# Two SwiGLU layers by seven block products: another order at the start of the second half's rows, and one set of slots for both phases

## The chip, the cores and the metric

One Trainium2 chip, one core of it. The metric is device time of one execution in microseconds (us); several runs give a median. The profile is one further execution, recorded by the hardware profiler; its times count from the start of its span.

## The reference

Two layers over a sequence of 1024 rows of 1024 features, batch 1, float32. Layer 0 mixes tokens by a gated delta rule, layer 1 by dilated windowed attention; each mixer and each FFN is preceded by an RMS norm with adaLN shift, scale and gate computed from `c`. The change touches the FFN of both layers:

```
def swiglu(h, w_in, w_out):
    gate, up = jnp.split(h @ w_in, 2, axis=-1)
    return (jax.nn.silu(gate) * up) @ w_out
```

with `FFN_HIDDEN` 2816 (22 tiles of 128), so `w_in` is 1024 x 5632 and `w_out` 2816 x 1024. The result is added to `x` under the gate of the adaLN.

## The kernel before, in words

A product of float32 numbers is made of three TensorE passes: each operand is split into a part `hi` (rounded to the matmul's type, a copy on ScalarE) and a part `lo` (the rest, a subtraction by `lo_of`, L164, given in turn to VectorE and GpSimd), and hi·hi, hi·lo and lo·hi are summed in PSUM. `hl` and `hx` are split rows, `w`, `wo` split weights.

**FFN-in.** The sequence is cut in two halves of 512 rows, the features (k) in 8 tiles of 128. For each hidden tile `i` of 22 the gate and the up columns times both halves would be eight block products of 4 k-tiles; the class `FfnIn` forms them from seven, in Winograd's way, `product(i, x)` with x = 1 to 7. Each is 4 k-tiles by 3 passes, 12 matmuls of 128x512. x = 1 and 2 need the first half's rows alone and the plain gate columns; x = 3 needs the plain second half (its k-tiles 4 to 7) and x = 4 to 7 need sums and differences of rows of both halves (`B[4]` to `B[7]`), which `half1` makes. The weights of x = 3, 5, 6, 7 are sums and differences of the raw columns (`weights`, L1209 to L1221), then split (`op`: ScalarE L1192, `lo_of` L164).

`begin` issues (0,1), (0,2), (1,1), (1,2). Then the second half's norm factor is made (a small matmul `pt`, VectorE L347, GpSimd L142, the broadcast matmul `pt`, the ScalarE copy `rb` L306) and `half1` multiplies the 8 k-tiles of the second half by it (L1156), applies the affine step on ScalarE (L1157), and forms `B[7]` (L1170, L1171), `B[6]` (L1176, L1178), `B[5]`, `B[3]`, `B[4]` in that order. `rest` then issues the products: 7, 6, 5 of tiles 0 and 1, then (0,3), (0,4), (2,1), (1,3), (1,4), then for each further tile 7, 6, 2, 5, next tile's 1, 3, 4. The order on TensorE within `begin` and `rest` is that of the program (`PE.pinned`); elsewhere a scheduler sets it, and every engine's queue, SP's DMA issues among them, runs in order.

`taken` gathers each product out of PSUM (L1244 to L1261), and the finished activations go to DRAM, `a_d`. In layer 0 `rest` calls `mods1` after nearly every product: it loads one 256 KB piece of layer 1's adaLN weights (`araw<-in_w_ada`, L226) and accumulates it on VectorE (L230).

**FFN-out.** `ffn_out` takes the hidden tiles in groups `FG` of 3, 4, 4, 4, 4, 3. For each group it loads the activations from `a_d` (L1289), splits them (`hl`, L1291), loads and splits `w_out` rows (`wunit`: L186 to L190, `w`), and makes 16 accumulations `pd` of 3 matmuls per tile of the group, each added to `x` by L1301. In both layers the pools of FFN-in (`hx` 12 buffers, `fw` 6 of `wo`, `ft`) are closed before those of FFN-out are opened, and all 16 tiles of `x` are loaded first (L1368 in layer 0).

Of the kernel before, what the change touches and what calls it, by code (L numbers as in the profile page):

```python
# [17 lines left out]
P = 128  # L18
# [53 lines left out]
def trunk(tc, A, out, stop=None):  # L72
# [236 lines left out]
    def make_h(p, l, w, xs, rb, aid=False, bufs=2):  # L309

        hs = []
        for k in range(KT):
            t = p.tile([P, HALF], F32, name="ht", tag="ht", bufs=bufs)
# [149 lines left out]
    class OutProj:  # L463
# [51 lines left out]
        def late(self, tp, w_from):  # L515
# [8 lines left out]
            stat = Stat(None, *(tp.tile([P, HALF], F32, name="sq", tag="ft") for _ in range(2)))  # L524
# [596 lines left out]
    class Slotted:  # L1121


        def __init__(self, p):
            self.p = p

        def take(self):
            return self.p.tile([P, HALF], F32, name="ft", tag="ft")
# [4 lines left out]
    class FfnIn:  # L1133
# [31 lines left out]
        def half1(self, xs, rb):  # L1165
            x0, x1, ft = self.x0, xs, self.ft
            for k in range(4):
                self.h(k, x1[k], rb)
                self.h(k + 4, x1[k + 4], rb)
                V.tensor_tensor(x0[k], x1[k], x0[k], ALU.subtract)  # L1170
                V.tensor_tensor(x1[k], x1[k + 4], x1[k], ALU.subtract)  # L1171
                self.B[7].append(self.pair(x1[k], True))
                ft.give(x1[k])
            for k in range(4):
                t = ft.take()
# [3 lines left out]
                ft.give(t)  # L1179
            for x, far, ts in ((5, True, x0[:4]), (3, False, x1[4:]), (4, False, x0[4:])):  # L1180
# [15 lines left out]
        def weights(self, i, x):  # L1196
            s, ft = self.st[i], self.ft
            if x in (1, 2):
                if x == 1:
                    s["rg"], s["ru"] = self.raw(i * P), self.raw(HID + i * P)  # L1200
                    w = s["w"] = wps.tile([P, 2, 1024], F32R, name="w", tag="w")
                    ACT.activation(w[:, 0], s["rg"], AF.Copy)
                    lo_of(w[:, 1], s["rg"], w[:, 0])
                c = slice((x - 1) * HALF, x * HALF)
                return s["w"][:, 0, c], s["w"][:, 1, c]
            a11, a12, a21, a22 = (t[:, j * HALF:(j + 1) * HALF] for t in (s["rg"], s["ru"]) for j in range(2))
            if x == 7:
                t = ft.take()
                V.tensor_tensor(t, a11, a21, ALU.subtract)  # L1209
                r = self.op(t)  # L1210
                ft.give(t)
            elif x == 6:
                s["s1"], s["s2"] = ft.take(), ft.take()
                G.tensor_tensor(s["s1"], a21, a22, ALU.add)
                V.tensor_tensor(s["s2"], s["s1"], a11, ALU.subtract)
                r = self.op(s["s2"])
            elif x == 5:
                r = self.op(s["s1"])
                ft.give(s["s1"])
            elif x == 3:  # L1220
                V.tensor_tensor(s["s2"], a12, s["s2"], ALU.subtract)  # L1221
                r = self.op(s["s2"])
                ft.give(s["s2"])
            else:
                r = self.op(a22)
            return r

        def product(self, i, x):
            s = self.st[i]
            wh, wl = self.weights(i, x)  # L1230
            key = {2: "y", 4: "v", 7: "v"}.get(x, "u")
            first, last = x in (1, 2, 7), x in (2, 3, 4)
# [7 lines left out]
        def taken(self, i, x, b):  # L1240
            s, ft = self.st[i], self.ft
            if x in (1, 6, 5):
                t = s["t%d" % x] = ft.take()
                ACT.activation(t, b, AF.Copy)  # L1244
                if x == 5:
                    V.tensor_tensor(t, s["v"], t, ALU.add)  # L1246
            elif x == 2:
# [3 lines left out]
            elif x == 3:  # L1251
                g = ft.take()
                ACT.activation(g, b, AF.Silu)
                G.tensor_tensor(s["t5"], s["t5"], g, ALU.mult)
                SP.dma_start(a_d[i, 1], s["t5"])
                ft.give(g, s["t5"])
# [7 lines left out]
        def begin(self):  # L1264
            for i in range(2):
                for x in (1, 2):
                    self.product(i, x)

        def rest(self, between=None):
            seq = [(i, x) for x in (7, 6, 5) for i in range(2)] + [(0, 3), (0, 4), (2, 1), (1, 3), (1, 4)]  # L1270
            for i in range(2, NHT):
                seq += [(i, 7), (i, 6), (i, 2), (i, 5)] + [(i + 1, 1)] * (i + 1 < NHT) + [(i, 3), (i, 4)]
# [7 lines left out]
    def ffn_out(l, xT, act_raw, tail):  # L1280

        w_o = A["w_ffn_out"][l]
        t0 = 0
        for gi, gn in enumerate(FG):
            wo, acts = [], [[], []]
            for t in range(t0, t0 + gn):
                for hf in range(2):
                    r = act_raw()
# [3 lines left out]
                    lo_of(lo, r, hi)  # L1292
                    acts[hf].append((hi, lo))
                wo.append(wunit(w_o[t * P:(t + 1) * P, None, :], 1))
            for hf in range(2):
                for n in range(KT):
                    o = pd()
                    split3(o, [((wo[i][0][:, 0, n * P:(n + 1) * P], wo[i][1][:, 0, n * P:(n + 1) * P]), acts[hf][i])
                               for i in range(gn)])
                    xt = xT[hf][n]  # L1300
                    V.scalar_tensor_tensor(xt, o, modT[:, l, 5, n:n + 1], xt, op0=ALU.mult, op1=ALU.add)  # L1301
                    if gi == len(FG) - 1:
                        tail(hf, n)
            t0 += gn

# [5 lines left out]
    def attn_weights(g, hq, kind):  # L1311
# [416 lines left out]
```

## Time and profile before

| | |
|---|---|
| median of 3 runs | 3078.36 us (3076.47 to 3082.93) |
| the profiled execution's own time | 3078.52 us |
| its span | 3076.7 us |
| mean granted TensorE clock | 0.945 |
| TensorE busy | 2793.5 us, 91% |
| VectorE, ScalarE, GpSimd busy | 53%, 34%, 32% |
| FFN-in, layer 0 and layer 1 | starts 850.77 and 2339.75, last product starts 1351.64 and 2809.05 |

The page of the profile gives busy time by engine and in 40 slices of the span, the granted TensorE clock of each slice (`PEclk`; 1.00 is 2.4 GHz, 0.50 is 1.2 GHz), the costliest groups of instructions and the DMA issues. The timeline lists consecutive instructions of one group on one engine: start, length, what they do, how many, and in brackets how long the engine stood idle before and what ended that. The end of a matmul is modelled, so the length of a PE row can reach past the next row's start; start to start is the safer reading. The windows view gives busy times, clock and DMA rate of a stretch, the waits view the idle time of an engine by what ended it. In the windows a bracket holds a count of instructions.

### The profile page before, as it was taken

What the parts mean: (1) busy time and instruction counts of PE and PEld (TensorE: products, weight loads), DVE (VectorE), ACT (ScalarE), POOL (GpSimd) and SP (SyncE); (2) the same over time, 40 slices, a digit from 0 to 9 for tenths busy, and PEclk for the clock granted to TensorE, in tenths of its full rate; (3) what the DMA queues carried; (4) which work ended last, traced back from release to release, by engine and by line L of the source; (5) the groups of instructions that cost most, each with busy time, mean ns of one, the idle gap of its engine ahead of it and who ended that gap; (6) DMA issues with size and microseconds to landing.
All of it is one profiled execution on the core that took longest, in us unless ns stands there. A gap on an engine that the chain in (4) does not pass through costs nothing.

```text
span 3076.7 us, 40439 instructions
## 1 busy us (share of the span) xinstructions
PE 2793.5 (91%) x15303; PEld 2372.6 (77%) x15303; DVE 1624.3 (53%) x3040; ACT 1058.5 (34%) x2097; POOL 995.9 (32%) x839
## 2 busy tenths in 40 slices
PE   6889888898949999969999999999975899998999
PEld 5777777776737787858889899999964688887887
DVE  7775576556666666435456342333377644344443
ACT  5432333333442333332124453443335333333210
POOL 2142323421253333433223132222224544444220
PEclk7989899999979999989999999999977999999999
DMA  7334332135705454244222411111231222226211
GB/s 250 97 94 120 95 86 66 55 101 187 236 25 159 148 164 154 83 162 136 79 79 65 107 42 35 50 49 47 80 107 58 82 83 82 82 90 213 95 52 55
DMA packets 301311, 311.78 MB, mean 101 GB/s; under 512 B 35011, under 2 KB 217539, under 8 KB 301116
## 3 DMA queue, kind: packets, MB, share of 16 engines
q1 hardware_dynamic: 293548, 289.30, 30.6%
q0 software_dynamic: 7568, 19.89, 2.0%
q8 instruction: 120, 1.97, 0.3%
q14 instruction: 75, 0.61, 0.1%
HBM read 250.16 MB, written 63.66 MB: 102 GB/s over the span
## 4 chain that ended last, share of the span: by engine, by line
PE 62%; DMA 11%; DVE 10%; POOL 6%; issue 4%; ACT 3%; SPq 0%; DVEq 0%; POOLq 0%; ACTq 0%
PE pd L82 33%; PE u L82 11%; PE v L82 5%; PE pt L82 4%; DMA araw<-in_w_ada 4%; PE y L82 3%; PE ob L82 2%; POOL U L805 2%; POOL Ut L803 2%; DVE acc L230 2%; DMA wraw<-in_gdn_w_in 1%; PE pp L82 1%; PE p L82 1%; DMA E<-gs_d 1%; PE sc L82 1%
## 5 line engine op out<-in xcount | busy, mean ns | idle before, releaser
L82 PE MATMUL pd<-hl,w 128*128 128x512 f32 x4248 | 1082.9, 409 | 53.9 <-ACT hl L1291 24.8
L82 PEld LDWEIGHTS pd<-hl,w 128*128 128x128 f32 x4248 | 807.2, 196 | 223.0 <-ACT hl L1291 25.6
L82 PE MATMUL pd<-w,hl 128*128 128x256 f32 x2880 | 377.4, 287 | 0.0
L82 PEld LDWEIGHTS pd<-w,hl 128*128 128x128 f32 x2880 | 355.8, 192 | 7.2 <-issue 5.9
L164 POOL TENSOR_TENSOR w<-wraw,w 128x1024 fp32r<-128x1024 f32 (+1 forms) x102 | 201.3, 1975 | 358.2 <-ACT w L190 247.4
L190 ACT ACTIVATE w<-wraw 128x512 fp32r<-128x512 f32 (+1 forms) x229 | 159.1, 710 | 299.2 <-DMA wraw<-in_gdn_w_in 98.2
L82 PE MATMUL u<-hx,wo 128*128 128x512 f32 x1056 | 255.7, 392 | 6.4 <-ACT wo L1192 4.5
L82 PEld LDWEIGHTS u<-hx,wo 128*128 128x128 f32 x1056 | 199.0, 189 | 49.1 <-ACT wo L1192 5.0
L164 DVE TENSOR_TENSOR w<-wraw,w 128x512 fp32r<-128x512 f32 (+1 forms) x160 | 154.5, 969 | 132.7 <-ACT w L190 117.2
L82 PE MATMUL v<-hx,wo 128*128 128x512 f32 x528 | 137.5, 411 | 81.0 <-ACT wo L1192 63.5
L82 PEld LDWEIGHTS v<-hx,wo 128*128 128x128 f32 x528 | 103.6, 199 | 108.1 <-ACT wo L1192 65.3
L230 DVE SCALAR_TENSOR_TENSOR acc<-araw,vecT,acc 128x512 f32<-128x512 f32 x140 | 133.9, 956 | 81.3 <-DMA araw<-in_w_ada 80.5
L82 PE MATMUL u<-hl,wo 128*128 128x512 f32 x528 | 129.7, 395 | 12.0 <-ACT ft L1244 8.2
L142 POOL TENSOR_TENSOR ssa<-ssa,pw 128x8 f32<-128x8 f32 x48 | 81.0, 1690 | 171.5 <-DVE ssa L1478 160.9
L1301 DVE SCALAR_TENSOR_TENSOR qkv<-pd,modT,qkv 128x512 f32<-128x512 f32 x96 | 71.5, 748 | 116.4 <-PE pd L82 116.2
L82 PE MATMUL u<-hl,w 128*128 128x512 f32 x528 | 127.2, 390 | 1.8 <-DVE qkv L490 1.8
L82 PE MATMUL v<-hl,wo 128*128 128x512 f32 x528 | 127.5, 391 | 0.7 <-DVE qkv L1246 0.7
L82 PE MATMUL y<-hl,w 128*128 128x512 f32 x528 | 127.1, 390 | 0.0
L82 PEld LDWEIGHTS u<-hl,wo 128*128 128x128 f32 x528 | 99.0, 189 | 36.3 <-ACT ft L1244 10.5
L1301 DVE SCALAR_TENSOR_TENSOR xt<-pd,modT,xt 128x512 f32<-128x512 f32 x96 | 71.2, 747 | 95.5 <-PE pd L82 95.1
L691 DVE SCALAR_TENSOR_TENSOR yv<-raw,vecT,yv 128x512 f32<-128x512 f32 x144 | 111.7, 776 | 12.9 <-ACT yv L689 11.7
L82 PEld LDWEIGHTS u<-hl,w 128*128 128x128 f32 x528 | 98.9, 188 | 22.6 <-issue 2.1
(364 smaller groups left out, 4321.4 us busy)
## 6 DMA issues: line engine op xcount, KB each, us to landing
araw<-in_w_ada SPq DMA_DIRECT2D x160, 256.0 KB, 2.8
wraw<-in_w_ffn_in SPq DMA_DIRECT2D x66, 512.0 KB, 4.3
wraw<-in_w_ffn_out SPq DMA_DIRECT2D x36, 512.0 KB, 4.5
wraw<-in_dsw_w_in SPq DMA_DIRECT2D x72, 256.0 KB, 2.8
wraw<-in_gdn_w_in SPq DMA_DIRECT2D x66, 256.0 KB, 2.9
a_d<-ft SPq DMA_DIRECT2D x44, 256.0 KB, 2.3
ar<-a_d SPq DMA_DIRECT2D x44, 256.0 KB, 4.9
qkv<-in_w_ffn_in SPq DMA_DIRECT2D x22, 512.0 KB, 4.0
```

Of the source, the lines that this page charges most:

```text
L82: i = f(*a, **k)
L142: G.tensor_tensor(o, i, pw[:, half, :n], ALU.pow)
L164: e.tensor_tensor(o, x, hi.bitcast(F32), ALU.subtract)
L190: ACT.activation(hi, raw, AF.Copy)
L230: V.scalar_tensor_tensor(acc, raw, condT[:, k:k + 1], acc, op0=ALU.mult, op1=ALU.add)
L691: V.scalar_tensor_tensor(yv, raw[:, i:i + HALF], convT[:, i, ct:ct + 1], yv, op0=ALU.mult, op1=ALU.add)
L803: G.tensor_tensor(t, U[:, 0:m, m:m + 1].to_broadcast([64, m, n]), U[:, m:m + 1, m + 1:32].to_broadcast([64, m, n]), ALU.mult)
L805: G.tensor_tensor(U[:, 0:m, m + 1:32], U[:, 0:m, m + 1:32], t, ALU.add)
L1301: V.scalar_tensor_tensor(xt, o, modT[:, l, 5, n:n + 1], xt, op0=ALU.mult, op1=ALU.add)
```

## The change

1. `begin` takes over the second half's norm and a third pair of products, (2,1) and (2,2), issued before any that needs the second half. The norm's first matmul comes after (1,2), the broadcast of its factor after (2,1). The gate columns for (2,1) come by a load of their own (`wr`, L1209 of the new file, into a `wo` slot).
2. The weights of (0,3), (1,3), (0,7), (1,7) are formed and split ahead of the second half's rows. The two weight sums `s1`, `s2` of a tile share a slot (`ss`, tag `wo`); differences of weights and rows use `sums` slots (layer 0: the 2 slots `araw`, which the adaLN pieces use too; layer 1: 5 slots `st`).
3. `half1` handles k-tiles 4 to 7 first and forms `B[3]` from them at once; the differences into `x0` move from VectorE (L1170 before) to GpSimd (L1177).
4. `rest` begins with (0,3), (1,3), each alone in its PSUM bank and held in SBUF until x = 5 is there, then 7, 6, 5, 4 of tiles 0 and 1. `mods1` is called after every second product only and goes on in `ffn_out`.
5. One pair of pools serves both phases: `fw` 16 buffers of `wo` (12 of them are the split rows `hx`, the rest are `op`, `ss`, `wr` and later the split `w_out`, as two 128x512 pieces by `wtwo`), `ft` 22. `x` is loaded tile by tile in the first group of `ffn_out`. `FG` becomes 2, 4, 4, 4, 4, 4. The number of matmuls and the bytes loaded stay as they were.

The diff, cut to its core:

```
         def half1(self, xs, rb):
...
+            for k in range(4, KT):
+                self.h(k, x1[k], rb)
+                self.B[3].append(self.pair(x1[k], False))
             for k in range(4):
                 self.h(k, x1[k], rb)
-                self.h(k + 4, x1[k + 4], rb)
-                V.tensor_tensor(x0[k], x1[k], x0[k], ALU.subtract)
-                V.tensor_tensor(x1[k], x1[k + 4], x1[k], ALU.subtract)
-                self.B[7].append(self.pair(x1[k], True))
+                t = sums.take()
+                V.tensor_tensor(t, x1[k + 4], x1[k], ALU.subtract)
+                self.B[7].append(self.pair(t, True))
+                sums.give(t)
+                G.tensor_tensor(x0[k], x1[k], x0[k], ALU.subtract)
...
-            for x, far, ts in ((5, True, x0[:4]), (3, False, x1[4:]), (4, False, x0[4:])):
+            for x, far, ts in ((5, True, x0[:4]), (4, False, x0[4:])):
...
+                    if i == 2:
+
+                        r = self.fw.tile([P, 1024], F32, name="wr", tag="wo")
+                        SP.dma_start(r.rearrange("p (k n) -> p k n", k=KT),
+                                     rows_cols(A["w_ffn_in"][self.l], i * P, P))
...
+            if x in (6, 5, 3) and "s1" not in s:
+                t = self.fw.tile([P, 2, HALF], F32, name="ss", tag="wo")
+                s["s1"], s["s2"] = t[:, 0], t[:, 1]
...
-        def begin(self):
-            for i in range(2):
-                for x in (1, 2):
-                    self.product(i, x)
+        def begin(self, factors, bcast):
+
+            for i in range(3):
+                self.product(i, 1)
+                if i == 2:
+                    rb = bcast(r)
+                self.product(i, 2)
+                if i == 1:
+                    r = factors()
+                    for j in ((0, 3), (1, 3), (0, 7), (1, 7)):
+                        self.ops[j] = self.weights(*j)
+            return rb
 
         def rest(self, between=None):
-            seq = [(i, x) for x in (7, 6, 5) for i in range(2)] + [(0, 3), (0, 4), (2, 1), (1, 3), (1, 4)]
+            seq = [(i, x) for x in (3, 7, 6, 5, 4) for i in range(2)]
...
-                if between is not None and n >= 8:
+                if between is not None and n >= 8 and n % 2:
                     between()
 
-    FG = [3, 4, 4, 4, 4, 3]
+    FG = [2, 4, 4, 4, 4, 4]
...
-            fw = f1.enter_context(pool("fw", 6))
-            tp = f1.enter_context(pool("ft", 18))
...
+        fw = fa.enter_context(pool("fw", 16))
+        tp = fa.enter_context(pool("ft", 22))
```

TensorE's queue at the start of layer 0's second half. Before:

```order
L82 MATMUL y<-hl,w 128x512 x12
L82 MATMUL pt<-sq 128x1 x4
L82 MATMUL pt<-sq,rst 128x128 x4
L82 MATMUL v<-hx,wo 128x512 x24
L82 MATMUL u<-hx,wo 128x512 x48
L82 MATMUL u<-hl,wo 128x512 x12
L82 MATMUL v<-hl,wo 128x512 x12
L82 MATMUL u<-hl,w 128x512 x12
```

And in the changed kernel:

```order
L82 MATMUL y<-hl,w 128x512 x12
L82 MATMUL pt<-sq 128x1 x4
L82 MATMUL u<-hl,w 128x512 x12
L82 MATMUL pt<-sq,ssx 128x128 x4
L82 MATMUL y<-hl,w 128x512 x12
L82 MATMUL y<-hl,wo 128x512 x24
L82 MATMUL v<-hx,wo 128x512 x24
L82 MATMUL u<-hx,wo 128x512 x48
```

The broadcast of the factor (`pt<-sq,ssx`) now stands behind (2,1) (`u<-hl,w`), and (2,2), (0,3), (1,3) (`y`) stand ahead of the first product that needs a difference of rows (`v<-hx,wo`).

SP's queue of DMA issues in the changed kernel, at the same place (`wraw` are the raw gate and up columns of hidden tiles 0, 0, 1, 1, 2, 2 in turn):

```order
L1193 DMA wraw_7276<-in_w_ffn_in 128x8x128
L1193 DMA wraw_7278<-in_w_ffn_in 128x8x128
L1193 DMA wraw_7313<-in_w_ffn_in 128x8x128
L1193 DMA wraw_7315<-in_w_ffn_in 128x8x128
L1193 DMA wraw_7707<-in_w_ffn_in 128x8x128
L1193 DMA wraw_7709<-in_w_ffn_in 128x8x128
L1209 DMA wr_7383<-in_w_ffn_in 128x8x128
L226 DMA araw_7704<-in_w_ada 128x512
```

There are four buffers of `wraw`, so the fifth and the sixth load wait until the sums of tile 0 have been formed on VectorE; the load `wr` that (2,1) needs stands behind both. VectorE's queue there (`araw` here holds a difference of weights):

```order
L1263 TENSOR_TENSOR ft<-y,ft 128x512
L1229 TENSOR_TENSOR araw<-wraw,ss 128x512
L164 TENSOR_TENSOR wo<-araw,wo 128x512
L1229 TENSOR_TENSOR araw<-wraw 128x512
L1263 TENSOR_TENSOR ft<-y,ft 128x512
L347 TENSOR_SCALAR ssx<-pt 128x4
L1229 TENSOR_TENSOR araw<-wraw 128x512
L164 TENSOR_TENSOR wo<-araw,wo 128x512
L1157 TENSOR_TENSOR xt<-xt,rb 128x512 x8
```

The last of these differences, that of (1,7), stands behind the norm's L347.

## Rows read from the trace of the kernel before

**Rows 1.** The page: busy time by engine, 40 slices, the granted clock.
```profile
PE 2793.5 (91%) x15303; PEld 2372.6 (77%) x15303; DVE 1624.3 (53%) x3040; ACT 1058.5 (34%) x2097; POOL 995.9 (32%) x839
PEclk7989899999979999989999999999977999999999
```

**Rows 2.** Timeline of PE, layer 0: start us, length, instruction, count [idle before <-releaser].
```profile
863.98 1.16 PE L82 MATMUL pt<-sq,rst 128*128 128x128 f32 x8 [1.38 <-POOL rst L142]
890.23 1.22 PE L82 MATMUL v<-hx,wo 128*128 128x512 f32 x2 [25.10 <-ACT wo L1192]
900.71 7.81 PE L82 MATMUL v<-hx,wo 128*128 128x512 f32 x22 [9.26 <-POOL wo L164]
908.36 2.88 PE L82 MATMUL u<-hx,wo 128*128 128x512 f32 x12
915.78 10.27 PE L82 MATMUL u<-hx,wo 128*128 128x512 f32 x36 [4.55 <-ACT wo L1192]
...
939.58 0.61 PE L82 MATMUL v<-hx,wo 128*128 128x512 f32 x2
```

**Rows 3.** Windows, layer 0's start: us, then busy us by engine, PEclk, DMA share, GB/s.
```profile
860.00:870.00 10.00, 3.76 (x24) 3.17 (x23) 5.05 (x9) 5.29 (x9) 1.68 (x2) 0.76 0.00 0
880.00:890.00 10.00, 0.00 (x0) 0.00 (x0) 10.00 (x9) 6.66 (x12) 8.17 (x6) 0.50 0.00 0
```

**Rows 4.** Timeline of VectorE, layer 0.
```profile
862.64 0.16 DVE L347 TENSOR_SCALAR rst<-pt 128x4 f32<-128x4 f32 x1 [5.11 <-PE pt L82]
865.80 5.98 DVE L1156 TENSOR_TENSOR xt<-xt,rb 128x512 f32<-128x512 f32 x8 [1.84 <-ACT rb L306]
...
878.06 0.68 DVE L1170 TENSOR_TENSOR xt<-xt 128x512 f32<-128x512 f32 x1
...
887.76 3.43 DVE L1209 TENSOR_TENSOR ft<-wraw 128x512 f32<-128x512 f32 x2
...
899.46 1.74 DVE L164 TENSOR_TENSOR wo<-ft,wo 128x512 fp32r<-128x512 f32 x1
```

**Rows 5.** Timeline of PE, layer 1.
```profile
2353.07 1.85 PE L82 MATMUL pt<-sq,ssx 128*128 128x128 f32 x8 [1.37 <-POOL ssx L142]
2385.49 1.22 PE L82 MATMUL v<-hx,wo 128*128 128x512 f32 x2 [30.57 <-ACT wo L1192]
...
2428.70 2.88 PE L82 MATMUL v<-hx,wo 128*128 128x512 f32 x12
```

**Rows 6.** Timeline of PE, from FFN-in to FFN-out: layer 0, then layer 1.
```profile
1378.58 10.98 PE L82 MATMUL pd<-hl,w 128*128 128x512 f32 x36 [24.06 <-ACT hl L1291]
...
2817.28 7.48 PE L82 MATMUL pd<-hl,w 128*128 128x512 f32 x24 [5.35 <-ACT w L190]
2825.47 1.19 PE L82 MATMUL pd<-hl,w 128*128 128x512 f32 x4 [0.72 <-ACT hl L1291]
2827.98 3.59 PE L82 MATMUL pd<-hl,w 128*128 128x512 f32 x8 [1.32 <-POOL hl L164]
2832.53 17.77 PE L82 MATMUL pd<-hl,w 128*128 128x512 f32 x77 [0.96 <-DVE qkv L1301]
```

**Rows 7.** Windows, FFN-in of both layers past its start, and layer 0's change of phase.
```profile
905.00:1352.00 447.00, 425.75 (x1875) 348.02 (x1875) 260.96 (x325) 143.75 (x237) 173.01 (x107) 0.98 0.42 129
2430.00:2809.00 379.00, 375.18 (x1651) 309.51 (x1651) 152.10 (x193) 133.09 (x214) 152.21 (x96) 1.00 0.29 92
1380.00:1390.00 10.00, 9.84 (x35) 7.63 (x34) 7.19 (x7) 7.79 (x12) 9.37 (x5) 0.80 1.04 396
```

**Rows 8.** DMA issues of the page: count, KB each, median us to landing.
```profile
wraw<-in_w_ffn_in SPq DMA_DIRECT2D x66, 512.0 KB, 4.3
```

**Rows 9.** Groups of instructions in 905 to 1352 us: count | busy us, mean ns.
```profile
L164 POOL TENSOR_TENSOR w<-wraw,w 128x1024 fp32r<-128x1024 f32 x20 | 48.9, 2446 | 84.1 <-ACT w L1202 74.2 <-DMA araw<-in_w_ada 5.3 <-DMA wraw<-in_w_ffn_in 4.6
L1202 ACT ACTIVATE w<-wraw 128x1024 fp32r<-128x1024 f32 x20 | 21.2, 1061 | 60.7 <-DMA wraw<-in_w_ffn_in 43.7 <-PE y L82 17.0
L230 DVE SCALAR_TENSOR_TENSOR acc<-araw,vecT,acc 128x512 f32<-128x512 f32 x84 | 91.0, 1083 | 44.4 <-DMA araw<-in_w_ada 43.8
```

More of the change, by code (lines that the diff above doesn't have):

```diff
@@ L523, in late @@
             rb0 = row_bcast(tp, self.r0, bufs=1)
-            stat = Stat(None, *(tp.tile([P, HALF], F32, name="sq", tag="ft") for _ in range(2)))
+            stat = Stat(None, *(tp.tile([P, HALF], F32, name="sq", tag="araw", bufs=2) for _ in range(2)))
             for n in range(KT):
@@ L1229, in product @@
             s = self.st[i]
-            wh, wl = self.weights(i, x)
+            wh, wl = self.ops.pop((i, x), None) or self.weights(i, x)
             key = {2: "y", 4: "v", 7: "v"}.get(x, "u")
-            first, last = x in (1, 2, 7), x in (2, 3, 4)
+            alone = i < 2 and x == 3
+            first, last = x in (1, 2, 7) or alone, x in (2, 3, 4) or (i < 2 and x == 5)
+            if alone:
+                key = "y"
             if first:
@@ L1251, in taken @@
             elif x == 3:
[L1252 to L1256, printed above, removed]
+                self.column(i, ft.take(), ft, b)
             elif x == 4:
@@ new lines, in wtwo @@
+    def wtwo(fw, raw, ap, a):
+        if a == 1:
+            SP.dma_start(raw, ap[:, 0])
+        else:
+            SP.dma_start(raw.rearrange("p (a b) -> p a b", a=a), ap)
+        ts = []
+        for i in range(2):
+            w, x = fw.tile([P, 2, HALF], F32R, name="w2", tag="wo"), raw[:, i * HALF:(i + 1) * HALF]
+            ACT.activation(w[:, 0], x, AF.Copy)
+            lo_of(w[:, 1], x, w[:, 0])
+            ts.append(w)
+        n = a // 2 if a > 1 else 4
+        return tuple(Two(*(w[:, j].rearrange("p (a b) -> p a b", a=n) for w in ts)) for j in range(2))
@@ L1302, in ffn_out @@
                     if gi == len(FG) - 1:
-                        tail(hf, n)
+                        tail(hf, n, xt)
+                    if between is not None and n % 2:
+                        between()
             t0 += gn
+        return xT
     def toks(g, t):
@@ new lines, in trunk, with mods1 @@
+        PE.pinned = True
+        rb = ff.begin(lambda: stat1.factors(ssx[:, :, 0:4]), lambda r: row_bcast(tp, r, bufs=1))
+        PE.pinned = False
+        ff.half1(xT[1], rb)
+        ends, calls = [], [0]
+        mods = [f for j in (1, 0, 2, 4, 3, 5)
+                for f in mod_pieces(tp, 1, j, lambda f: ends.append((calls[0] + 2, f)), "ft")]
+        def mods1():
+            calls[0] += 1
+            while ends and ends[0][0] <= calls[0]:
+                ends.pop(0)[1]()
+            if mods:
+                mods.pop(0)()
@@ new lines, in trunk, with tail0 @@
+        PE.pinned = True
+        ff.rest(mods1)
+        PE.pinned = False
+        banks(pd="ab", pt="de", p0="a", p1="b", p2="c")
+        stat = [Stat(None, None, None) for _ in range(2)]
+        rb = [None, None]
+        xT = [[], []]
+        def tail0(hf, n, x):
+            while n == 0 and (mods or ends):
+                mods1()
+            if n == 0:
+                stat[hf].acc = ft.take()
+            stat[hf].sqx = ft.take()
+            stat[hf].add(x)
+            xT[hf].append(x)
@@ L1692, in tail1 @@
                     PE.transpose(b[:, i * P:(i + 1) * P], xT[hf][n - 3 + i][:, j * P:(j + 1) * P], ident)
-                ot = tp.tile([P, HALF], F32, name="yo", tag="ft")
+                ot = sums.take()
                 if j % 2:
```

190 lines of the change are left out of this document (86 added, 104 removed).

## The prediction, made before the change was run

> **What bounds the kernel now.** I read the page first: TensorE is busy 91% of the span, no other engine over 53% [rows 1], so what can be won is TensorE's idle time and its low clock. The clock row of the 40 slices dips at four places within the FFNs [rows 1], and the timeline of TensorE shows each as gaps: the start of the second half's rows in either layer, and the change from FFN-in to FFN-out in either layer. The price of work comes from a stretch at full clock: 1651 matmuls in 375.18 us [rows 7] are 0.227 us each, 2.73 us for a product of 12.
>
> *Start, layer 0.* The norm's factor is in use on VectorE at 865.80 [rows 4]. TensorE then stands idle 25.10, 9.26 and 4.55 us [rows 2], released each time by a split on ScalarE or GpSimd, that is, by operands not yet made. (1,4) ends where (2,7) starts, at 939.58 [rows 2]: 73.8 us for 11 products, 30.0 us of work. The loss, 43.8 us, is the 38.9 us of idle time and the low clock around it: TensorE was granted 0.50 at 880 to 890, with VectorE busy all 10.00 us and GpSimd 8.17 [rows 3]. So VectorE and GpSimd bound this stretch, and together they are slow: a VectorE subtraction takes 0.68 us alone (at 878.06) and 1.7 us beside GpSimd (two in 3.43 at 887.76, 1.74 at 899.46) [rows 4].
>
> *Start, layer 1.* The same form: idle 30.57 us after the broadcast at 2353.07, (1,4) ends at 2428.70 [rows 5].
>
> *Change of phase, layer 0.* Idle 24.06 us until the first split activation, then 36 matmuls in 10.98 us, where 8.2 would do [rows 6]: 26.9 us lost. *Layer 1:* gaps of 5.35, 0.72, 1.32 and 0.96 us, and 7.48, 1.19 and 3.59 us for 24, 4 and 8 matmuls worth 5.4, 0.9 and 1.8 [rows 6]: 12.4 us lost.
>
> *Steady part.* Layer 0 has 447.00 - 425.75 = 21.3 us of idle TensorE in 905 to 1352, layer 1 only 3.8 us in its 379 [rows 7].
>
> **The change, part by part.**
>
> *The start, layer 0.* The new queue puts (2,1), (2,2), (0,3), (1,3) ahead of anything that needs differences of rows. But (2,1) needs its own load `wr`, and SP issues that behind two loads that wait for weight differences on VectorE, the last of which stands behind the norm's L347. L347 runs at 862.64 [rows 4] and two subtractions of 0.68 follow it or stand around it, so `wr` goes out at about 864.2. Its landing takes 4.3 us in the median [rows 8], with the DMA idle there [rows 3]: 868.5 to 869. ScalarE's copy is 1.06 us, GpSimd's lo part 2.45 us [rows 9]; they end near 872.5, (2,1) on a slow clock at about 876.5, since it can end only after the lo part. The broadcast now stands behind (2,1) on TensorE: with its 1.16 us [rows 2] and the copy `rb` (0.6 us, as between the broadcast's end and 865.80) the factor is in use at about 878.5 in place of 865.80. This is a new wait of 12.7 us, and all of `half1` is queued behind it.
>
> From the factor on, the amount of VectorE and GpSimd work is nearly the old one, in another order. Before, (0,6) started at 908.36, 42.6 us after the factor [rows 2, 4]. Of what VectorE did by then, the weight differences (3.43 us) and a split of one (1.74) [rows 4] now lie ahead of the factor, so `B[6]` and the weights of (0,6) should be there about 37 us after it. By then (2,2), (0,3), (1,3), (0,7), (1,7) can have run: `B[3]` needs 8 multiplications (5.98 us [rows 4]) and four pairs. Behind (0,6) remain six products, 16.4 us. So (1,4) ends 53.4 us after the factor, at 931.9, with 12 products done ((2,2) among them). Before, the same 12 would be done at 939.58 + 2.73 = 942.3. Gain **10.4 us**. Bounds: 23 us if `wr` comes in time (865.8 + 53.4 = 919.2); nothing, if the two slots of `sums` in layer 0 let each difference start only after the split before it.
>
> The four subtractions into `x0` go from VectorE to GpSimd. By the rows a pair of one VectorE and one GpSimd instruction takes 1.7 us, so in the worst case a moved one adds 1.0 us to VectorE's neighbour, 4 us in all; GpSimd had 1.8 us of 10 free at 880 [rows 3] and more before, so I add nothing. The Trainium skill's "SBUF — State Buffer", section "SBUF: two separate sides", says that VectorE and GpSimd hold their shared port pair as an exclusive lock for a whole instruction, the loser blocking fully; by that rule the move only swaps a shorter hold for a longer one, and a reader who goes by it would take some 3 us off each layer's gain and come out near 3021.
>
> *The start, layer 1.* The differences have five slots there, and none waits behind the norm, so `wr` can be issued some 5 us before L347 and be there in time. The factor is then late only by (2,1) and its lo part, about 4.4 us: 2360 in place of about 2355.6 (the broadcast at 2353.07, its 1.85 us [rows 5] and the copy). With the same 53.4 us the 12 products are done at 2413.4, before at 2428.70 + 2.73 = 2431.4. Gain **18 us** (10 to 24).
>
> *Change of phase, layer 0.* No pool is closed, so `w_out` of the first two groups and most loads run under the last products, and the first `hl` waits only for its place on ScalarE behind a weight piece that takes the slot freed by the last product. I count 1.5 us of idle time, some 3 us of low clock and 2.5 us for late inputs of the second group, 7 us of the 26.9: gain **20 us** (15 to 24). The cover is the first group, 96 matmuls or 21.8 us; in it 16 tiles of `x` (4.2 MB) and the next group's weights and activations (4.2 MB) are to land, 21.5 us at the 396 GB/s seen here [rows 7]. It just fits; with adaLN pieces in between it would not quite, and the stall is the few us counted.
>
> *Change of phase, layer 1.* The scheduler puts the first `pd` between the last three products; I leave 2.4 us of 12.4: gain **10 us** (6 to 12).
>
> *Steady part, layer 0.* The adaLN pieces are 91.0 of VectorE's 261 us there [rows 7, 9]; half go to FFN-out, beside matmuls, where they cost nothing as long as each addition to `x` keeps ahead of TensorE. With VectorE freer some of the 21.3 us should go: gain **5 us** (-15 to 12). The same matmuls, bytes and activations remain; two half-size weight copies in place of one lie beside matmuls and cost nothing.
>
> Sum: 10.4 + 18 + 20 + 10 + 5 = 63 us. The profiled execution took 3078.5 us, 0.2 us over the median of the runs, so no correction is needed: 3078 - 63 = **3015 us**.
>
> **The rivals.**
>
> *A, slots too few (slower).* For the split weights `wo` had 6 buffers; of the 16 now 12 hold `hx`, which leaves four, and `ss` takes one from x = 6 to x = 3. In layer 0 the differences share two `araw` slots with adaLN pieces, for whose landing VectorE already stood idle 43.8 us [rows 9]. If in each of 20 tiles of each layer one weight is late by 2.5 us (about what a difference, its copy and its split take beyond the cover), that is 40 x 2.5 = 100 us: 3115 us. It decides from 63 / 40 = 1.6 us a tile on. For it: layer 0 had such waits even with six buffers. Against it: three buffers hold the weights of two coming products, 5.5 us of cover, and layer 1 ran with 3.8 us idle in all [rows 7]. The Trainium skill's "Perfetto Trace Analysis", section "Identifying the Most-Contended Engine", reads a gap that repeats through a stretch as a sign that there is no SBUF for the next tile; before, no such repeated gap shows in layer 1.
>
> *B, the start wins little.* The factor is later than I think, or VectorE and GpSimd in step take as long as before: 0 in layer 0, 8 in layer 1; the phases give 15 + 8, the steady part nothing: 31 us, 3047 us. For it: the stretch is bound by these two engines and their work is hardly less.
>
> *C, all of it.* `wr` is not late, the changes of phase nearly vanish: 23 + 24 + 24 + 11 + 12 = 94 us, 2984 us. For it: the matmuls put first cover 13.7 us of the dead time; against it SP's order.
>
> *D, it does not do what it says:* the four gaps are only moved, with stalls in the steady part giving back the rest; 3078 us.
>
> **How the numbers follow.** My forecast 0.49 (3000 to 3032), B 0.19, C 0.17, A 0.11, D 0.04. The range reaches from the middle of C to beyond B, 2985 to 3058; A and half of C are left out, about 0.2. A measurement tells about 0.2% (6 us; the runs differ by 6.5). Faster: forecast, B and C, 0.85; same 0.04 (D); slower 0.11 (A).
>
> **What would show it.** In the changed profile: (2,1) of layer 0 starting near 870 and the multiplications by the factor near 878; (1,4) ending near 932 and 2413 with the same point of departure; the first `pd` within 2 us of the last product in layer 0 and none of the 5.35 us in layer 1; TensorE's idle time in the middle of layer 0's FFN-in at or below 21 us. The forecast is wrong if TensorE shows a repeated wait on `wo` in either steady part (A), or if (0,6) starts 42 us or more after the factor (B).

## The result, and the profile after

The changed kernel takes 3023.8 us in the median of 4 runs (3023.06 to 3028.07), the kernel before 3077.99 us (3076.47 to 3082.93): a ratio of 0.9824, 95% interval 0.9807 to 0.9841, 54 us faster. Forecast were 3015 us, 2985 to 3058. The profiled execution took 3023.1 us, its span is 3021.3 us, 55.4 us under the span before. The page shows the same matmuls, with less idle time and a higher clock (0.955 for 0.945) [rows 1]:

```profile
PE 2799.0 (93%) x15303; PEld 2373.6 (79%) x15303; DVE 1607.3 (53%) x3055; ACT 1067.9 (35%) x2139; POOL 998.1 (33%) x866
PEclk8989999999989999999999999999968899999999
```

Where the 55.4 us came from, from the starts of the same products on TensorE in both timelines. "Start" is the time from the start of (1,2) to the end of twelve products ((2,1), (2,2) and x = 3 to 7 of tiles 0 and 1); where (2,2) comes later than (1,4) its 2.73 us are added.

| place | before | after | gain | forecast |
|---|---|---|---|---|
| up to layer 0's (0,1) | 850.8 | 843.2 | 7.6 | 0 |
| start, layer 0 | 83.4 | 75.3 | 8.1 | 10.4 |
| twelfth product to the last one, layer 0 | 409.3 | 402.8 | 6.5 | 5 |
| change of phase, layer 0 (loss) | 26.9 | 7.2 | 19.7 | 20 |
| FFN-out of layer 0, attention, to layer 1's (1,2) | 966.6 | 979.1 | -12.5 | 0 |
| start, layer 1 | 83.4 | 68.0 | 15.4 | 18 |
| rest of FFN-in, change of phase and end, layer 1 | | | 10.4 | 10 |

Each column is one profiled execution. Three kernels below have the same start with an edit elsewhere (pieces at every product, old groups, `x` loaded first): there it took 73.8, 76.6 and 77.4 us in layer 0 and 66.3, 66.1 and 63.2 us in layer 1. So a difference between two starts of up to 4 us, in layer 1 up to 5, shows nothing by itself.

TensorE at the start of layer 0, to be held against [rows 2]:

```profile
862.78 1.22 PE L82 MATMUL u<-hl,w 128*128 128x512 f32 x2 [7.74 <-ACT w L1215]
865.20 3.88 PE L82 MATMUL u<-hl,w 128*128 128x512 f32 x10 [1.20 <-POOL w L164]
868.92 1.05 PE L82 MATMUL pt<-sq,ssx 128*128 128x128 f32 x8
...
886.82 5.83 PE L82 MATMUL y<-hl,wo 128*128 128x512 f32 x14 [2.82 <-POOL hl L164]
892.49 5.60 PE L82 MATMUL v<-hx,wo 128*128 128x512 f32 x24
902.25 1.22 PE L82 MATMUL u<-hx,wo 128*128 128x512 f32 x2 [4.16 <-ACT wo L1198]
907.58 12.94 PE L82 MATMUL u<-hx,wo 128*128 128x512 f32 x46 [4.12 <-DVE wo L164]
```

The single gap of 25.10 us is now filled with (2,1), (2,2), (0,3), (1,3), in pieces. But the broadcast `pt<-sq,ssx` comes late. The same stretch on all other engines shows why:

```profile
853.11 3.16 SPq L1193 DMA_DIRECT2D wraw<-in_w_ffn_in  x2
...
855.08 0.16 DVE L347 TENSOR_SCALAR ssx<-pt 128x4 f32<-128x4 f32 x1
855.16 0.68 DVE L1229 TENSOR_TENSOR araw<-wraw 128x512 f32<-128x512 f32 x1
...
856.32 0.58 SPq L1209 DMA_DIRECT2D wr<-in_w_ffn_in  x1
...
861.67 1.06 ACT L1215 ACTIVATE w<-wr 128x1024 fp32r<-128x1024 f32 x1 [5.17 <-DMA wr<-in_w_ffn_in]
862.80 2.35 POOL L164 TENSOR_TENSOR w<-wr,w 128x1024 fp32r<-128x1024 f32 x1 [6.06 <-ACT w L1215]
...
870.64 4.90 DVE L1157 TENSOR_TENSOR xt<-xt,rb 128x512 f32<-128x512 f32 x8 [13.41 <-ACT rb L306]
```

The load `wr` is issued after the last weight difference (L1229) has run, lands 5 us later, and the factor is in use 19.3 us after the start of (1,2). Before it was 6.9 us (858.93 to 865.80): 12.4 us late, forecast 12.7.

TensorE from FFN-in to FFN-out, layer 0, and the interleaved first additions of layer 1, against [rows 6]:

```profile
1329.47 2.88 PE L82 MATMUL v<-hl,wo 128*128 128x512 f32 x12
1336.56 35.69 PE L82 MATMUL pd<-hl,w 128*128 128x512 f32 x144 [4.20 <-ACT hl L1345]
...
2764.32 1.69 PE L82 MATMUL pd<-hl,w 128*128 128x512 f32 x6 [2.86 <-DVE qkv L1358]
2765.83 4.57 PE L82 MATMUL u<-hl,wo 128*128 128x512 f32 x12
```

24.06 us of idle time became 4.20, and 144 matmuls then run through. In layer 1 a wait of 2.86 us and one slow product (4.57 us) remain.

### The profile page after: what moved, and what is told of

Its sections match the earlier page's. It is cut to its first block, busy times and chain, and to the rows that moved or that the text cites. A ratio compares the mean times of both kernels' runs of the same rounds, so it can differ in the third digit from the quotient of the medians.

```text
span 3021.3 us, 40540 instructions
## 1 busy us (share of the span) xinstructions
PE 2799.0 (93%) x15303; PEld 2373.6 (79%) x15303; DVE 1607.3 (53%) x3055; ACT 1067.9 (35%) x2139; POOL 998.1 (33%) x866
## 4 chain that ended last, share of the span: by engine, by line
PE 67%; DVE 10%; DMA 10%; POOL 4%; issue 3%; ACT 3%; SPq 0%; DVEq 0%; POOLq 0%; ACTq 0%
PE pd L82 33%; PE u L82 13%; PE v L82 6%; PE pt L82 5%; DMA araw<-in_w_ada 4%; PE y L82 3%; PE ob L82 3%; POOL U L805 1%; POOL Ut L803 1%; PE pp L82 1%; DVE acc L230 1%; DMA wraw<-in_gdn_w_in 1%; PE sc L82 1%; DVE w L164 1%; DMA E<-gs_d 1%
## 5 line engine op out<-in xcount | busy, mean ns | idle before, releaser
L164 POOL TENSOR_TENSOR w<-wraw,w 128x512 fp32r<-128x512 f32 (+1 forms) x109 | 188.7, 1735 | 329.0 <-ACT w L190 159.0
L190 ACT ACTIVATE w<-wraw 128x512 fp32r<-128x512 f32 (+1 forms) x171 | 107.8, 645 | 218.3 <-DMA wraw<-in_gdn_w_in 101.3
L142 POOL TENSOR_TENSOR ssa<-ssa,pw 128x8 f32<-128x8 f32 x48 | 80.7, 1683 | 170.1 <-DVE ssa L1536 160.7
L1358 DVE SCALAR_TENSOR_TENSOR qkv<-pd,modT,qkv 128x512 f32<-128x512 f32 x96 | 71.0, 747 | 117.8 <-PE pd L82 117.8
L82 PE MATMUL u<-hl,wo 128*128 128x512 f32 x480 | 120.8, 402 | 7.7 <-ACT ft L1255 7.7
L82 PE MATMUL v<-hx,wo 128*128 128x512 f32 x528 | 126.8, 390 | 0.1
L82 PEld LDWEIGHTS v<-hl,wo 128*128 128x128 f32 x528 | 99.4, 189 | 21.9 <-DVE ft L1257 1.1
L1578 DVE CUSTOM_DVE_ANT_0 p<-pt,bias 128x256 f32<-128x256 f32 (+1 forms) x192 | 61.6, 369 | 102.0 <-PE pt L82 63.4
L82 PEld LDWEIGHTS u<-hl,wo 128*128 128x128 f32 x480 | 92.5, 194 | 29.6 <-ACT ft L1255 9.9
```

Of the source, the lines that this page charges most:

```text
L82: i = f(*a, **k)
L142: G.tensor_tensor(o, i, pw[:, half, :n], ALU.pow)
L164: e.tensor_tensor(o, x, hi.bitcast(F32), ALU.subtract)
L190: ACT.activation(hi, raw, AF.Copy)
L1578: V.tensor_tensor_reduce(p_[i][:, hp, c0:], lg[i][:, hp * 256 + c0:hp * 256 + 256], bias[:, h, c0:], 1.0, -3.0e38, ALU.add, ALU.max, orow[ ...
```

## The experiments

Each kernel is the changed one with the edit shown, unless it says otherwise. Times are medians of 4 runs (5 for the last), ratios those to the kernel before on the same chip.

### The late factor

Broadcast ahead of (2,1):

```
             for i in range(3):
-                self.product(i, 1)
                 if i == 2:
                     rb = bcast(r)
+                self.product(i, 1)
                 self.product(i, 2)
```

> Edit: in begin the broadcast of the second half's factor stands ahead of (2,1) on TensorE, so the factor no longer waits for the late load wr. Read from the changed kernel's trace: relative to the start of (1,2) the factor is in use 12.4 us later than in the kernel before in layer 0, and the broadcast starts 7.1 us later in layer 1. Theory (the late factor is paid in full, since VectorE and GpSimd work without a break from the factor on): most of 12.4 + 7.1 comes back, 3004 to 3012 us, and the broadcast of layer 0 follows (1,2) by about 5 us. Rival (the wait is hidden, the start is bound by TensorE's products or by the weight sums): 3024 us within 4.

3001.8 us (2999.2 to 3004.6), ratio 0.9748 (0.9733 to 0.9762). The starts took 61.7 us (75.3 in the changed kernel) and 61.9 us (68.0). TensorE in layer 0, with (1,2) at 844.45:

```profile
849.87 1.96 PE L82 MATMUL pt<-sq,ssx 128*128 128x128 f32 x8 [1.75 <-POOL ssx L142]
856.26 1.22 PE L82 MATMUL u<-hl,w 128*128 128x512 f32 x2 [4.43 <-ACT w L1215]
...
885.02 1.22 PE L82 MATMUL u<-hx,wo 128*128 128x512 f32 x2 [4.00 <-ACT wo L1198]
```

The broadcast follows (1,2) by 5.4 us instead of 17.5, and every later product moves up with it. (2,1) waits for its load just as before, but now in time in which TensorE would mostly have waited for `half1` anyway: (0,7), the first product that needs a difference of rows, starts 22.9 us after the factor, 21.9 in the changed kernel. In layer 0 the wait was paid in full.

The load `wr` ahead of the raw columns of tile 1, TensorE's order as changed:

```
             for i in range(3):
+                if i == 1:
+                    self.wr = self.fw.tile([P, 1024], F32, name="wr", tag="wo")
+                    SP.dma_start(self.wr.rearrange("p (k n) -> p k n", k=KT),
+                                 rows_cols(A["w_ffn_in"][self.l], 2 * P, P))
                 self.product(i, 1)
...
```

> Edit: the order on TensorE stays, but the load wr is issued ahead of the raw columns of hidden tile 1, so it lands before (2,1) is due. Theory: (2,1) follows (1,2) at once and the factor is late only by (2,1) itself, about 3 us in either layer in place of 12.4 and 7.1: 3009 to 3016 us. Rival (order on TensorE and not the load makes the factor late, or the wait is hidden): 3020 to 3028 us.

3006.5 us (3003.4 to 3010.6), ratio 0.9765 (0.9749 to 0.9781); starts 65.0 and 61.8 us. The place of the load in SP's queue was what made the factor late; the gain is a little over the theory's.

The third pair put back behind (0,5), (1,5), all else at the start as changed:

```
-            for i in range(3):
+            for i in range(2):
...
-            seq = [(i, x) for x in (3, 7, 6, 5, 4) for i in range(2)]
+            seq = [(i, x) for x in (3, 7, 6, 5) for i in range(2)] + [(2, 1), (0, 4), (1, 4)]
...
```

> Edit: (2,1) and (2,2) go back behind the first products that need the second half; weights ahead, B[3] first and (0,3), (1,3) first stay; the factor is broadcast right after (1,2). Theory: the factor comes 12.4 and 7.1 us earlier, two products of 2.73 us move out of dead time in each layer: 3024 - 19.5 + 11 = 3015, between 3010 and 3020 us: as placed, the third pair costs more than it gives. Rival (the wait is hidden and the third pair fills dead time): 3024 + 11 = 3035 us.

3019.0 us (3013.9 to 3022.9), in the theory's span. Starts, with (2,2) added: 68.7 us (75.3) and 66.8 us (68.0). Without the pair layer 0's start is shorter: as placed it cost more there than it gave. Layer 1's difference is within what the same start varies by. Against this kernel, the same pair with the broadcast ahead of it is worth 7.0 us in layer 0 and, less surely, 4.9 in layer 1 (61.7 and 61.9).

### The start as a whole

Both starts as in the kernel before, pools and phases as changed:

```
-            for i in range(3):
+            for i in range(2):
...
-                    for j in ((0, 3), (1, 3), (0, 7), (1, 7)):
-                        self.ops[j] = self.weights(*j)
...
-            for k in range(4, KT):
-                self.h(k, x1[k], rb)
-                self.B[3].append(self.pair(x1[k], False))
...
-            seq = [(i, x) for x in (3, 7, 6, 5, 4) for i in range(2)]
+            seq = [(i, x) for x in (7, 6, 5) for i in range(2)] + [(0, 3), (0, 4), (2, 1), (1, 3), (1, 4)]
...
```

> Edit: the start of both layers as in the kernel before (two pairs ahead, no weights ahead, half1 and the order of the first products as before); the shared slots, the one-by-one loads of x, the groups and the rarer adaLN pieces stay. Theory (the start gave 8 us in layer 0 and 15 us in layer 1, of which about 5 us were lost again just ahead of layer 1's FFN by weight sums on VectorE and GpSimd): 3024 + 23 - 5 = 3042, between 3038 and 3048 us. Rival (the change of phase gives little by itself and the start is where the gain is): 3060 us or more.

3035.2 us (3024.3 to 3036.6), below the theory's span of 3038 to 3048 and far from the rival's 3060. The starts are 78.0 and 82.9 us (83.4 and 83.4 before), so layer 1's is back and layer 0's is not quite; the gap at layer 0's change of phase stays closed (2.5 us idle), and the 4.6 us stall ahead of layer 1's FFN is gone (1.9 us). So all of the change but the start, the rarer adaLN pieces included, brings some 40 us. The new start adds only 11 us to that: in the profiles it is 2.7 and 14.9 us shorter, but the stretch from layer 0's first `pd` to layer 1's (1,2) takes 981.9 us instead of 975.3.

### The change of phase

Old groups:

```
-    FG = [2, 4, 4, 4, 4, 4]
+    FG = [3, 4, 4, 4, 4, 3]
```

> Edit: groups of hidden tiles in FFN-out 3, 4, 4, 4, 4, 3 again, pools and loads as in the changed kernel. Theory (what closed the gap is that loads and splits run ahead under the last products; the size of the first group only helps): the idle time ahead of the first pd of layer 0 grows from 4.2 us to 5 to 9 us, the whole 3024 to 3032 us. Rival (the small first group is what closed the gap): the gap is back to 15 us or more and the whole at 3036 us or more.

3021.3 us (3013.1 to 3024.5); 3.6 us between the last product and the first `pd` (4.4 in the changed kernel by the same count). Both ends of the theory's range were too high: the groups show no effect.

All 16 tiles of `x` of layer 0 loaded first:

```
+        if l == 0:
+            for hf in range(2):
+                for n in range(KT):
+                    xT[hf].append(ft.take())
+                    SP.dma_start(xT[hf][n], xs_d[hf, n])
...
-                    if gi == 0:
+                    if gi == 0 and l == 1:
```

> Edit on the changed kernel: in layer 0 all 16 tiles of x are loaded ahead of the first group of FFN-out again; pools and groups stay as changed. Theory (the gap closed because the first activations no longer stand behind 16 loads on SP, which issue over 10 us, and behind slots that come free with the last products): the gap ahead of the first pd grows from 4.4 us to 10 to 18 us, the whole 3030 to 3040 us. Rival (not closing the pools is enough, since all loads run ahead): the gap stays under 6 us, 3024 within 4.

3029.3 us (3027.0 to 3034.3), a shade under the theory's span, with the gap as it said. TensorE, then SP's queue:

```profile
1349.29 20.90 PE L82 MATMUL pd<-hl,w 128*128 128x512 f32 x84 [16.76 <-ACT hl L1350]
```

```profile
1338.69 4.25 SPq L1341 DMA_DIRECT2D ft<-xs_d  x7
1343.24 1.68 SPq L1348 DMA_DIRECT2D ft<-a_d  x3
```

The first activations are issued at 1343.24, behind the 16 loads, which begin at 1330.30; in the changed kernel four of them go out at 1329.75, ahead of any `x`. So of the 20 us won here some 12.5 hang on the order of the loads on SP, not on the pools being open. The whole grew by 5.5 us only; in this profile layer 1's start, whose code is unchanged, took 63.2 us instead of 68.0, which hides part of it.

### The adaLN pieces

```
-                if between is not None and n >= 8 and n % 2:
+                if between is not None and n >= 8:
```

> Edit: the adaLN pieces of layer 1 are taken up after every product of layer 0 again, not after every second. In the changed kernel the stretch from the twelfth product to the last one of layer 0's FFN-in is 6.7 us shorter than before, of which 2.4 us are small matmuls that only moved to FFN-out. Theory (fewer pieces on VectorE and fewer loads in the two shared slots gave the rest): the stretch gets 4 to 12 us longer, the first matmuls of FFN-out lose their 3 us of waits, the whole 3024 to 3034 us. Rival (the pieces are hidden either way): 3024 within 3 us. Rival (the two shared slots stall every tile as soon as both are wanted): over 3040 us.

3029.6 us (3028.6 to 3033.9), as the theory said, but as the difference of two larger numbers: from the twelfth product to the last of layer 0 it takes 420.4 us instead of 402.8 (17.6 more, where 4 to 12 were expected), and from the first `pd` to layer 1's (1,2) 974.5 instead of 981.9 (7.4 less). The windows of that first stretch, this kernel and the changed one, show 8.1 us more matmul time, of which 2.0 are the small ones that had moved out, and 22.8 instead of 12.9 us idle:

```profile
924.00:1344.00 420.00, 397.25 (x1741) 322.70 (x1740) 261.67 (x315) 138.99 (x228) 169.09 (x105) 0.98 0.45 142
```

```profile
927.00:1329.00 402.00, 389.13 (x1714) 320.13 (x1713) 226.07 (x287) 138.97 (x227) 164.21 (x104) 0.98 0.43 133
```

### Too few slots: my slower rival, with fewer still

In both layers:

```
-        fw = fa.enter_context(pool("fw", 16))
+        fw = fa.enter_context(pool("fw", 15))
...
-        ff.fw = fw = fa.enter_context(pool("fw", 16))
+        ff.fw = fw = fa.enter_context(pool("fw", 15))
```

> Edit: 15 slots instead of 16 in the shared pool of both layers, so three are left beside the split rows, one of them held by the weight sums for most of a tile. My rival of too few slots, tested by making them fewer. Theory (four slots leave a product of slack, three leave almost none): repeated waits of TensorE on weights appear in both steady parts, 1 to 2.5 us a tile, 40 to 100 us in all, 3064 to 3124 us. Rival (slots are not what the products wait for): 3024 to 3032 us.

3038.2 us (3028.2 to 3045.8), some 14 us slower, between the two. Not by repeated waits: layer 0's stretch after the twelfth product takes 401.0 us (402.8), layer 1's 389.7 (385.1). The starts lose 4.1 and 3.7 us, a little more than they vary by, and 4.4 us go between layer 0's last product and layer 1's (1,2). Even with three slots TensorE is not held up tile by tile in layer 0:

```profile
engine line waited for: us in total, times, longest us
PE u L82 <- ACT ft L1255: 5.4, 7, 2.3
PE u L82 <- ACT wo L1198: 3.4, 1, 3.4
PE u L82 <- POOL wo L164: 1.0, 3, 0.4
```

(Waits of TensorE, 933 to 1336 us.) In layer 1, from 2400 to 2788 us, the same view has three waits, 5.7 us in all.

### VectorE and GpSimd

The subtractions into `x0` back on VectorE:

```
-                G.tensor_tensor(x0[k], x1[k], x0[k], ALU.subtract)
+                V.tensor_tensor(x0[k], x1[k], x0[k], ALU.subtract)
```

> Edit: the four subtractions into x0 of each layer are given back from GpSimd to VectorE. By the rows (both engines take turns, a pair 1.7 us, so a moved instruction costs the same turn): each start within 2 us of the changed kernel, the whole 3024 within 4 us. By the rule of an exclusive lock held for a whole instruction (a GpSimd subtraction of 1.28 us holds VectorE off longer than one of 0.6 us on VectorE itself): each start 2 to 4 us shorter, 3016 to 3020 us. Rival (GpSimd was the idle one and VectorE the bound): each start 2 to 4 us longer, 3028 to 3032 us.

3019.4 us (3015.4 to 3023.8): by the total not to be told from the changed kernel, nor by the starts, 74.6 us (75.3) and 66.3 us (68.0). What the move does to VectorE and GpSimd shows in the time from the factor's first use to (0,6). With the subtractions on GpSimd it is 31.6 us in layer 0 and 30.5 to 30.6 in layer 1, in the changed kernel and in the three others with its start alike; here it is 29.9 and 27.9:

```profile
874.35 4.91 DVE L1157 TENSOR_TENSOR xt<-xt,rb 128x512 f32<-128x512 f32 x8 [14.67 <-ACT rb L306]
```

```profile
904.24 1.22 PE L82 MATMUL u<-hx,wo 128*128 128x512 f32 x2 [6.83 <-ACT wo L1198]
```

That is 1.7 and 2.6 us, nearer to the rule of the lock than to "the same turn"; how much of it reaches the end of the start is not shown.

The three edits together (broadcast first, early `wr`, `x0` on VectorE):

> Edits of three runs together: broadcast ahead of (2,1), the load wr ahead of the raw columns of tile 1, the subtractions into x0 on VectorE. Theory: the broadcast gives what it gave alone (3002 us), VectorE's subtractions another 2 us in each start (72.9 and 66.3 us against 75.3 and 68.0 in the changed kernel), the early load little, since (2,1) stands in dead time: 2992 to 3000 us. Rival (they hide one another): 3000 to 3006 us.

3001.6 us (2995.5 to 3004.5), ratio 0.9759 (0.9742 to 0.9776), no better than the broadcast alone. Starts 66.0 and 58.6 us: layer 1 gains 3.3, layer 0 loses 4.3. TensorE in layer 0, where the broadcast alone had 1.75 us of idle time, then VectorE and GpSimd:

```profile
861.65 2.08 PE L82 MATMUL pt<-sq,ssx 128*128 128x128 f32 x8 [4.09 <-POOL ssx L142]
```

```profile
852.77 2.87 DVE L1227 TENSOR_TENSOR araw<-wraw,ss 128x512 f32<-128x512 f32 x1 [0.63 <-POOL wo L164]
```

```profile
852.70 2.39 POOL L164 TENSOR_TENSOR w<-wr,w 128x1024 fp32r<-128x1024 f32 x1
858.50 1.65 POOL L164 TENSOR_TENSOR wo<-araw,wo 128x512 fp32r<-128x512 f32 x1 [3.40 <-ACT wo L1198]
860.12 1.48 POOL L142 TENSOR_TENSOR ssx<-ssx,pw 128x4 f32<-128x4 f32 x1
```

The early split of `wr` has ended 5 us before the factor's L142, so it does not hold it up directly, although what I expected of the last run, below, says so. Beside it a weight difference takes 2.87 us on VectorE instead of 0.69, and the next weight's split, which stands ahead of L142 on GpSimd, comes later by that. The broadcast is late by 2.3 us; that this is the layer's whole loss is not shown, for the next kernel, with the same code in layer 0 and the same wait, took 61.8 us there.

The stall ahead of layer 1's FFN in the changed kernel. TensorE, VectorE, GpSimd:

```profile
2308.76 4.44 PE L82 MATMUL u<-hl,w 128*128 128x512 f32 x12 [4.58 <-DVE qkv L490]
```

```profile
2291.76 4.50 DVE L340 TENSOR_TENSOR qkv<-qkv 128x512 f32<-128x512 f32 x1
...
2301.61 5.74 DVE L340 TENSOR_TENSOR qkv<-qkv 128x512 f32<-128x512 f32 x1
```

```profile
2291.95 1.29 POOL L164 TENSOR_TENSOR hl<-qkv,hl 128x512 fp32r<-128x512 f32 x1
2293.18 1.28 POOL L1225 TENSOR_TENSOR ss<-wraw 128x512 f32<-128x512 f32 x1
2294.41 1.29 POOL L164 TENSOR_TENSOR hl<-qkv,hl 128x512 fp32r<-128x512 f32 x1
...
2301.97 2.39 POOL L164 TENSOR_TENSOR w<-wraw,w 128x1024 fp32r<-128x1024 f32 x1
2304.32 1.26 POOL L1225 TENSOR_TENSOR ss<-qkv 128x512 f32<-128x512 f32 x1
2305.54 1.25 POOL L164 TENSOR_TENSOR wo<-st,wo 128x512 fp32r<-128x512 f32 x1
```

An addition that takes 0.68 us elsewhere (L340) lasts until GpSimd's run of three has ended, and the weight sums L1225 are what makes two runs into runs of three. Behind it stand the additions L490 that free TensorE's banks. Without weights ahead in layer 1 (on the combined kernel):

```
-                    for j in ((0, 3), (1, 3), (0, 7), (1, 7)):
+                    for j in ((0, 3), (1, 3), (0, 7), (1, 7)) if self.l == 0 else ():
```

> Edit on the combined kernel: in layer 1 the weights of (0,3), (1,3), (0,7), (1,7) are not formed ahead. Theory (the weight sums on GpSimd, queued back to back with other work, held up a VectorE addition for 4.50 and 5.74 us and with it the additions that free TensorE's banks): the 4.6 us of idle time ahead of layer 1's (0,1) fall to 2 us or less and (0,1) runs at full clock, 4 to 6 us back; the start after (1,2) gets 3 to 6 us longer, since the weights are then formed in it: within 4 us of the combined kernel. Rival (the stall has another cause): it stays at 4.6 us and the kernel is 3 to 6 us slower.

3008.6 us (3005.6 to 3013.6). The stall falls to 1.42 us and (0,1) runs at full clock, as the theory had it. But the start of layer 1 grows from 58.6 to 76.0 us, where 3 to 6 were expected: all its products wait, since the first, (0,3), cannot begin before its weights are split on ScalarE, behind `half1`:

```profile
2335.01 4.50 PE L82 MATMUL y<-hl,wo 128*128 128x512 f32 x12 [29.61 <-ACT wo L1198]
```

Weights ahead are thus worth 17 us in layer 1 and cost about 5. Last, both: broadcast first, `x0` on VectorE, `wr` as late as changed, and the sums `s1` of tiles 0 and 1 of layer 1 on VectorE:

```
-                G.tensor_tensor(s["s1"], a21, a22, ALU.add)
+                (V if self.l == 1 and i < 2 else G).tensor_tensor(s["s1"], a21, a22, ALU.add)
```

> Edits on the changed kernel: broadcast ahead of (2,1), the subtractions into x0 on VectorE, wr as late as in the changed kernel (loaded early, its lo part on GpSimd held up the factor's L142 in layer 0: 4.09 us of idle time ahead of the broadcast instead of 1.75), and the sums s1 of tiles 0 and 1 of layer 1 on VectorE, so that fewer GpSimd instructions stand back to back beside VectorE's L340. Theory: the idle time ahead of layer 1's (0,1) falls from 4.6 to 3 us or less; from the start of (1,2) to the end of (1,4) 59 to 61 us in layer 0 and 58 to 60 us in layer 1; the whole 2992 to 2999 us. Rival (the stall ahead of layer 1 is VectorE's own work and not GpSimd's runs): it stays at 4.6 us or grows, 2998 to 3004 us.

3000.5 us (2998.3 to 3006.5), ratio 0.9762 (0.9746 to 0.9778). The stall is down to 0.83 us and the longest L340 in that stretch to 1.77, so with the sums off GpSimd the stall goes. Putting `x0` on VectorE or the broadcast first had left it at 4.6 us, so GpSimd's runs were its cause:

```profile
2295.24 2.97 PE L82 MATMUL u<-hl,w 128*128 128x512 f32 x12 [0.83 <-DVE qkv L490]
```

```profile
2283.47 1.77 DVE L340 TENSOR_TENSOR qkv<-qkv 128x512 f32<-128x512 f32 x1
```

Starts 63.5 and 58.6 us. In the total it lies where the broadcast alone lies, above the theory's 2999: 3.78 us of idle time stand ahead of the norm of layer 1's first half, behind a VectorE addition, and the layer 0 start is 1.8 us longer. Whether the edits cause these two is not shown. Three kernels, 3000.5, 3001.6 and 3001.8 us, beat the changed one by some 22 us and cannot be told apart.

## Why the prediction was right, and where its steps were off

**Right in the main.** 3015 was forecast, 3023.8 measured. Each of the four places gave what its term said, within 3 us (layer 1's change of phase by itself some 8 of 10, for of the 12.4 us lost the wait of 2.86 us and the slow product remain). The terms together miss by 3 us; the other 5 are the two rows of the table that had no term, 7.6 and -12.5. The largest risk named in the order of the queues, `wr` behind the weight differences, came as worked out (12.4 us late in layer 0 for 12.7), and moving the broadcast shows that it was paid in full. Two signs that were named did not come: the first `pd` of layer 0 followed the last product by 4.4 us, not 2, and layer 1 kept a gap.

**Start, layer 0: 10.4 forecast, 8.1 measured.** Mis-sized was the stretch from the factor to the end of (1,4): 56.0 us (870.64 to 926.7) for 53.4. (0,6) began 31.6 us after the factor rather than 37, but the six products from it on took 24.4 us instead of 16.4, with 4.12 us of idle time inside (0,6) and a granted clock of 0.51 from 902 to 912. That the two nearly cancel is luck, and 2.3 us are within what this start varies by. The step "so I add nothing" for the four subtractions on GpSimd failed: up to (0,6) they cost 1.7 us here and 2.6 in layer 1. The Trainium skill's "SBUF — State Buffer", section "SBUF: two separate sides", by which a GpSimd instruction shuts VectorE out while it lasts, came nearer here, but the 3 us that the prediction made of it were too much.

**Start, layer 1: 18 forecast, 15.4 measured.** The term "be there in time" for `wr` failed: TensorE waited 1.56 us for its copy and 1.70 for its lo part, and the broadcast came 7.1 us later than before, not 4.4. With the same start the other three profiles gained 17.1, 17.3 and 20.2 us, so the size of this term stands.

**Change of phase, layer 0: 20 and 19.7.** The size was right, the reason only in part: I named the pools; the order of the loads on SP makes 12.5 of it, and the small first group none. The 7 us that I left were 1.5 of idle time, 3 of low clock and 2.5 of late inputs; they came as 4.20 of idle time and 3 of low clock, so their sum was luck in part. (The cover sum there, 8.4 MB at 396 GB/s, is 21.2 us and not 21.5, which changes nothing.) The late inputs of the second group did not show; 2.97 us of waits for VectorE's additions (L1358) came later in FFN-out instead.

**Steady part: 5 and 6.5.** Here two numbers were hidden in one. "Half go to FFN-out, where they cost nothing" failed: taking them back makes FFN-in 17.6 us longer and the stretch behind it 7.4 us shorter. And with as many pieces as before the stretch takes 420.4 us, 11.1 more than in the kernel before (409.3): by these profiles the rest of the change costs the steady part that much, and the rarer pieces more than pay for it. What costs it (the weight differences now share two slots with the pieces) was not tried by itself.

**Left out altogether.** Weights ahead were priced only by what they take off the start. What they put onto GpSimd ahead of layer 1's FFN, and the 4.58 us of idle time with a low clock behind it, was in no term: 2.8 us more idle time than before, and 1.4 us more for (0,1). With the 7.4 us of the adaLN pieces this makes up most of the -12.5 us in the table. On the other side layer 0's FFN began 7.6 us earlier. TensorE's order up to there is the same in both kernels, and among the changed kernel and the edits of it (0,1) started anywhere from 836.3 to 846.2 us, so this is about the scatter of that stretch. Why it lies below the 850.8 of the kernel before each time stays open.

**The rivals.** A, too few slots, is refuted with a slot to spare: with three instead of four the loss is 14 us and shows no repeated gap in either layer. The sentence on repeated gaps that the prediction takes from the Trainium skill's "Perfetto Trace Analysis" stands in its section "Optimization Strategy" and says only that such a gap can mean too little room; here a slot less cost time without one. B and C bounded the truth from both sides; C's first two terms, 23 and 24 us with the factor in time, nearly came true when the broadcast went first (21.7 and 21.5).

## What to carry to other kernels

When work is moved into dead time, look at what it is put in front of on the in-order queues: a filler that waits for its own load was harmless behind the norm's broadcast and made the factor 12 us late ahead of it. The first loads of a new phase belong ahead of bulk loads that are needed later; here that alone was 12.5 us of TensorE's idle time. Work that is cheap by its own duration can be dear by where it stands: weights ahead were worth 17 us at one place and cost 5 at another. And before a difference of 2 us between two profiles is believed, look at a third with the same code in that stretch.

## What the runs showed of the hardware that was not expected

VectorE's addition L340, 0.68 us alone, did not take turns with GpSimd but outlasted a whole run of GpSimd instructions standing back to back: 4.50 us beside three of 1.28, and 5.74 us beside 2.39 + 1.26 + 1.25. A weight difference, 0.69 us alone, took 2.87 beside one split of 2.39. In other places of the same kernels the two engines alternate, 1.7 us a pair [rows 4]. What decides between the two was not tried.
